# The retention branch of a hybrid decoder trunk: chunks of 64 tokens in place of 128

## The chip, the cores and the metric

The kernel runs on one core of a Trainium2 chip. The metric is device time in microseconds for one launch: the whole trunk, two layers, from the first instruction to the last. Three runs of the kernel before took 1705.79 to 1705.82 us, with a median of 1705.8 us. The engines are TensorE (PE, with PEld for its weight loads), VectorE (DVE), ScalarE (ACT), GpSimd (POOL) and SyncE (SP), which issues the DMAs.

## The reference, cut to what matters

Each layer normalizes `x`, projects it once into four causal mixers (forgetting attention, gated linear attention "GLA", retention, Mamba-2 "SSD") and a gate for each, sums the gated mixers, projects the sum out, and follows with a SwiGLU block. Sequence length is 512, the model width 1024. The change concerns retention alone: four heads of 64, float32.

```python
def retention_chunked(q, k, v, log_gamma):          # CHUNK = 64
    scores = einsum('bcthd,bcshd->bchts', qf, kf) * decay
    o_intra = einsum('bchts,bcshv->bcthv', scores, vf)
    kv = einsum('bcshd,sh,bcshv->bchdv', kf, k_w, vf)
    def step(state, kv_c):
        return state * chunk_decay[:, None, None] + kv_c, state
    _, s_in = lax.scan(step, s0, moveaxis(kv, 1, 0))
    o_inter = einsum('bcthd,th,bchdv->bcthv', qf, q_w, s_in)
    return o_intra + o_inter
```

The decay of retention is a fixed power of a constant per head, so the same output comes from chunks of any length: within a chunk by masked scores, across chunks by a state that is decayed and added to once per chunk.

## The kernel before

Everything is feature-major: 128 partitions hold features (or, in value tiles, tokens), 512 tokens lie along the free axis. Four heads of 64 are two pairs `j`, and `half` is the head within the pair, so that a head lies on 64 of the 128 partitions.

The large projections (`w_in`, the gates, the up projections, `w_out`, both halves of the SwiGLU) are split into a high and a low part in a one-pass float format, and each block of 128x128 weights takes three matmuls (`mm3`, by L200 `mm`). Their weights arrive in slabs of eight blocks by DMA, are cast by ACT (`wh`, L214) and subtracted by DVE (`wl`, L215). A slab's buffers come free when the last matmul on the slab three before has run.

The small matmuls of the mixers read float32 tiles directly. A float32 matmul takes two passes of the array, and each pass has a record of its own in the trace. Matmuls whose operands lie on 64 partitions use half of the array's rows; those that write 64 partitions of PSUM use half of its columns.

The four mixers are generators (`ssd`, `gla`, `ret`, `fox`) that `drain` runs one after the other. At each `yield` the drain emits projection work from a list (`fill`) worth some microseconds, so that projections stand between the dependent steps of a mixer. From this order of emission a scheduler with a simulated timeline sets the order of instructions on each engine when the program is built. On the chip each engine keeps that order and waits on semaphores.

Retention in the kernel before, in four chunks of 128 tokens:

- rotary: `rq` and `rk` are turned (L936 to L940).
- scores: sixteen matmuls per layer, each 64 features deep, 128 keys by 128 queries. DVE multiplies four tiles of 128x512 by a decay table out of PSUM (L957).
- keys to token-major: eight transposes (L964), times a decay (L966).
- contributions: twelve matmuls per layer, 128 tokens deep, 64x64 out, into one PSUM tile for three chunks.
- states: two copies (L980) and two steps of four scalar_tensor_tensor instructions on 64x64 (L983) write three states to `sbd`.
- output: sixteen value matmuls (128 tokens deep, 64 by 128 out) and then six matmuls of the state (128 deep, 128x128, both heads of a pair at once by a block-diagonal `sbd`) onto the same PSUM tiles. Both are called "inter" and "values" below: values are `v` times scores, inter is state times decayed query (`qd`).
- `headnorm` squares, sums, normalizes and multiplies by the gate.

GLA, which runs just before, is written in chunks of 64 already: 28 contributions of 64x64, seven states by L902 and L905, and inter matmuls on 64x64.

Of the kernel before, what the change touches and what calls it, by code (L numbers as in the profile page):

```python
# [14 lines left out]
ALU = mybir.AluOpType  # L15
# [3 lines left out]
P = 128  # L19
# [3 lines left out]
NB = S // P  # L23
# [3 lines left out]
NH = 4  # L27
# [28 lines left out]
def _const_parts():  # L56
# [4 lines left out]
    for m in range(P):  # L61
        if m % 64 < 32:
            perm[m + 32, m] = -1.0
        else:
            perm[m - 32, m] = 1.0
    dret = np.zeros((P, NH, P))
    rel = i[None, :] - i[:, None]
    for h in range(NH):
        dret[:, h, :] = np.where(rel >= 0, np.exp(np.maximum(rel, 0) * LOGG[h]), 0.0) * 0.125
    qdec = np.zeros((P, 2, P))  # L70
    for j in range(2):
        for half in range(2):
            qdec[64 * half:64 * half + 64, j, :] = np.exp((i + 1.0) * LOGG[2 * j + half])[None, :]
    kdec = np.exp((P - 1.0 - i)[:, None] * LOGG[None, :]) * 0.125
    inv = (10000.0 ** (-np.arange(32) / 32.0))[i % 32][:, None]
# [59 lines left out]
def trunk(ctx: ExitStack, tc: tile.TileContext, keys, qkeys, xin, pos, wst, wsq, par, ext, cst, out):  # L135
# [54 lines left out]
    def MX():  # L190
        return px.tile([P, S], F32, tag="mx", name=nm("mx"))
# [4 lines left out]
    def chunked(ap, n=NB):  # L196
        return ap.rearrange("p (c t) -> p c t", c=n)

    def mm(o, l, r, start, stop):
        T.matmul(o, lhsT=l, rhs=r, start=start, stop=stop, skip_group_check=True)  # L200
# [140 lines left out]
    def C(n):  # L341
        o, w = CONST_OFF[n]
        return cs[:, o:o + w]
# [10 lines left out]
    Uf = U.bitcast(F32)  # L354
    dret = C("dret").rearrange("p (h t) -> p h t", h=NH)
    qdec = C("qdec").rearrange("p (h t) -> p h t", h=2)
# [94 lines left out]
    def layer(l, n1, scope):  # L451
# [175 lines left out]

        def headnorm(pos_, gain, gates_, res):
            sq = []
# [15 lines left out]
            for j, t in enumerate(r):  # L645
                act(out=t, in_=t, func=AF.Exp, scale=-0.5)
                newton(t, pn[j], 64)
                V.scalar_tensor_tensor(out=t, in0=pos_[j], scalar=gain, in1=t, op0=ALU.mult, op1=ALU.mult)
                V.tensor_tensor(out=t, in0=t, in1=gates_[j], op=ALU.mult)
                res[j] = split_tile(t)  # L650
# [276 lines left out]
        def ret():  # L927
# [15 lines left out]
            for j in range(2):  # L943
                t = TT()
                G.tensor_tensor(out=chunked(t), in0=chunked(rq[j]), in1=qdec[:, j].unsqueeze(1).broadcast_to([P, NB, P]), op=ALU.mult)
                qd.append(t)
            ms = {}
            for j in range(2):
                pa = [MX(), MX()]
                for tb in range(NB):  # L950
                    ts = slice(tb * P, (tb + 1) * P)
                    for half in range(2):
                        hs = slice(64 * half, 64 * half + 64)
                        mm(pa[half][:, ts], rk[j][hs, ts], rq[j][hs, ts], True, True)
                for half, ps in enumerate(pa):
                    t = TT()
                    V.tensor_tensor(out=chunked(t), in0=chunked(ps), in1=dret[:, 2 * j + half].unsqueeze(1).broadcast_to([P, NB, P]), op=ALU.mult)  # L957
                    ms[j, half] = t
                yield
            kt = []  # L960
# [7 lines left out]
            yield  # L968
            ps = MX()
            pv = ps[:, :384].rearrange("p (c j n) -> p c j n", c=3, j=2)  # L970
            for c in range(3):
                for j in range(2):
                    for half in range(2):
                        hd = 2 * j + half
                        mm(pv[64 * half:64 * half + 64, c, j], kt[j][:, c * P + 64 * half:c * P + 64 * half + 64], rv[0][:, c, hd * 64:(hd + 1) * 64], True, True)
            for c in range(3):
                for half in range(2):
                    hs = slice(64 * half, 64 * half + 64)
                    if c == 0:
                        V.tensor_copy(out=sbd[hs, 0, :, hs], in_=pv[hs, 0])  # L980
                    else:
                        for j in range(2):
                            V.scalar_tensor_tensor(out=sbd[hs, c, j, hs], in0=sbd[hs, c - 1, j, hs], scalar=float(np.exp(P * LOGG[2 * j + half])), in1=pv[hs, c, j], op0=ALU.mult, op1=ALU.add)  # L983
            yield
            pos_ = [MX(), MX()]
            for j, po in enumerate(pos_):
                for c in range(NB):
                    ts = slice(c * P, (c + 1) * P)
                    for half in range(2):
                        hd = 2 * j + half  # L990
                        mm(po[64 * half:64 * half + 64, ts], rv[0][:, c, hd * 64:(hd + 1) * 64], ms[j, half][:, ts], c == 0, False)
            for j, po in enumerate(pos_):
                for c in range(1, NB):
                    ts = slice(c * P, (c + 1) * P)
                    mm(po[:, ts], sbd[:, c - 1, j], qd[j][:, ts], False, c == NB - 1)
            yield
            yield from headnorm(pos_, PR("rn"), gates["r"][2:], yc)


# [553 lines left out]
```

## Time and profile before

| | |
|---|---|
| median of 3 runs | 1705.8 us |
| the profiled execution, whole | 1704.74 us |
| span of its instructions | 1703.0 us |
| PE busy in the span | 1695.2 us |
| DVE busy | 1213.9 us |
| ACT busy | 862.3 us |
| granted TensorE clock, mean | 1.000 |

The profiled execution's own time is 1.7 us more than its span and 1.1 us less than the median of the timed runs. A row of the timeline gives the start of an instruction or of a run of like instructions, how long it lasted to the modelled end of the last, and in brackets the idle time before it on its engine. Matmuls are pipelined: the distance between two starts is what the array took, the duration beside it is longer and overlaps the next. Layer 0's retention runs at 255 to 271 us, layer 1's at 1101 to 1117 us.

### The profile page before, as it was taken

To read this page: it belongs to the slowest core of one execution; us is meant where nothing else is said; L and a number is where in the kernel's file an instruction comes from. 1 tells how busy PE (TensorE), PEld (TensorE's weight loads), DVE (VectorE), ACT (ScalarE), POOL (GpSimd) and SP (SyncE) were. 2 spreads that over 40 slices of the span, in tenths; PEclk is the share of its full clock that TensorE was granted. 3 is DMA by queue.
4 is the path that set the end of the run, shared out by engine and by line. 5 is a ranking of instruction groups with operands and counts; after the bars stand their busy time and mean duration, and the time that the engine had idled before them with its cause. 6 is when DMAs were issued, how large, how long until landed. Compare 5 with 4: busy or idle time off the path is not lost.

```text
span 1703.0 us, 25205 instructions
## 1 busy us (share of the span) xinstructions
PE 1695.2 (100%) x10174; PEld 1476.3 (87%) x10174; DVE 1213.9 (71%) x1692; ACT 862.3 (51%) x1188; POOL 218.1 (13%) x221
## 2 busy tenths in 40 slices
PE   9999999999999999999999999999999999999999
PEld 8878888888888999998988788888888889999998
DVE  6867676777677676676777766767776677767666
ACT  5425543546357555464544354435554474655543
POOL 3021220022101010101020212201221010101010
PEclk9999999999999999999999999999999999999999
DMA  6322222222235657575333222322222366665743
GB/s 208 112 72 73 80 75 87 87 87 76 86 99 159 181 135 190 130 192 117 89 108 112 64 75 76 98 76 87 79 83 87 99 176 161 152 175 138 189 105 108
DMA packets 54838, 195.02 MB, mean 115 GB/s; under 512 B 6208, under 2 KB 6848, under 8 KB 54720
## 3 DMA queue, kind: packets, MB, share of 16 engines
q1 hardware_dynamic: 45936, 161.93, 30.2%
q0 software_dynamic: 8640, 31.46, 10.3%
q8 instruction: 80, 1.31, 0.3%
q14 instruction: 38, 0.31, 0.1%
q10 hardware_dynamic: 144, 0.00, 0.0%
HBM read 191.28 MB, written 2.10 MB: 114 GB/s over the span
## 4 chain that ended last, share of the span: by engine, by line
PE 97%; DVE 2%; ACT 1%; issue 1%; POOL 0%; DVEq 0%; POOLq 0%
PE mm L200 65%; PE mx L200 31%; PE mx L1092 1%; DVE t L846 0%; DVE f L1436 0%; DVE x L1437 0%; ACT wh L214 0%; DVE wl L215 0%; PE mx L702 0%; DVE t L852 0%; ACT t L238 0%; DVE t L380 0%; ACT L233 0%; ACT g L238 0%; DVE t L1181 0%
## 5 line engine op out<-in xcount | busy, mean ns | idle before, releaser
L214 ACT CAST wh<-wr 128x1024 fp32r<-128x1024 f32 (+1 forms) x239 | 250.1, 1047 | 359.3 <-PE mm L200 200.1
L200 PE MATMUL mm<-xh,wh 128*128 128x512 f32 (+1 forms) x1184 | 428.4, 362 | 1.4 <-DVE t L1181 0.9
L200 PE MATMUL mm<-xh,wl 128*128 128x512 f32 (+1 forms) x1184 | 427.6, 361 | 0.0
L200 PE MATMUL mm<-xl,wh 128*128 128x512 f32 (+1 forms) x1184 | 427.4, 361 | 0.0
L215 DVE TENSOR_TENSOR wl<-wr,wh 128x1024 fp32r<-128x1024 f32 (+1 forms) x219 | 283.7, 1296 | 108.6 <-ACT wh L214 106.5
L200 PEld LDWEIGHTS mm<-xh,wh 128*128 128x128 f32 x1184 | 222.5, 188 | 36.1 <-DVE t L1181 1.8
L200 PEld LDWEIGHTS mm<-xl,wh 128*128 128x128 f32 x1184 | 222.4, 188 | 34.5 <-issue 1.5
L200 PEld LDWEIGHTS mm<-xh,wl 128*128 128x128 f32 x1184 | 222.5, 188 | 33.9 <-issue 0.6
L200 PE MATMUL mm<-t,wh 128*128 128x512 f32 x448 | 140.3, 392 | 0.0
L200 PE MATMUL mx<-xl,wh 128*128 128x256 f32 (+1 forms) x448 | 137.8, 309 | 0.0
L200 PE MATMUL mx<-xh,wh 128*128 128x256 f32 (+1 forms) x448 | 135.3, 310 | 0.0
L1300 POOL DMA_DIRECT2D wl<-in_wsq_dram x60 | 51.9, 864 | 517.4 <-ACT wl L1299 384.0
L200 PE MATMUL mx<-f,wh 128*128 128x512 f32 x352 | 108.2, 390 | 0.0
L200 PE MATMUL mm<-f,wh 128*128 128x512 f32 (+1 forms) x360 | 106.4, 385 | 0.0
L200 PEld LDWEIGHTS mm<-t,wh 128*128 128x128 f32 x448 | 83.2, 188 | 17.3
L215 DVE TENSOR_TENSOR l<-rq,wh 128x1024 fp32r<-128x1024 f32 x60 | 73.2, 1220 | 32.5 <-ACT wh L214 18.6
L200 PE MATMUL mx<-xh,wl 128*128 128x256 f32 (+1 forms) x288 | 91.2, 327 | 0.0
L200 PEld LDWEIGHTS mx<-xh,wh 128*128 128x128 f32 x448 | 84.2, 188 | 5.2 <-ACT wh L214 0.2
L200 PEld LDWEIGHTS mx<-xl,wh 128*128 128x128 f32 x448 | 84.1, 188 | 5.1
L200 PE MATMUL mm<-t,wl 128*128 128x512 f32 x224 | 87.4, 390 | 0.0
L214 ACT CAST wh<-rq 128x1024 fp32r<-128x1024 f32 x60 | 62.9, 1049 | 43.8 <-PE mm L200 21.5
L200 PEld LDWEIGHTS mm<-f,wh 128*128 128x128 f32 x360 | 67.1, 188 | 13.3
(277 smaller groups left out, 3431.2 us busy)
## 6 DMA issues: line engine op xcount, KB each, us to landing
wr<-in_wst_dram SPq DMA_DIRECT2D x217, 512.0 KB, 3.5
rq<-in_wsq_dram SPq DMA_DIRECT2D x60, 512.0 KB, 5.6
wl<-in_wsq_dram POOLq DMA_DIRECT2D x60, 512.0 KB, 7.2
wr<-in_wsq_dram SPq DMA_DIRECT2D x20, 512.0 KB, 6.7
out_dram<-x SPq DMA_DIRECT2D x7, 256.0 KB, 2.1
x<-in_x_dram SPq DMA_DIRECT2D x3, 512.0 KB, 7.9
x<-in_x_dram SPq DMA_DIRECT2D x2, 256.0 KB, 4.0
wr<-in_wst_dram SPq DMA_DIRECT2D x2, 256.0 KB, 4.2
```

The source lines that it names most:

```text
L200: T.matmul(o, lhsT=l, rhs=r, start=start, stop=stop, skip_group_check=True)
L214: seen["copy"] = A.copy(out=hi, in_=src)
L215: V.tensor_tensor(out=lo, in0=src, in1=hi.bitcast(F32), op=ALU.subtract)
L1092: T.transpose(ps[:, W:W + P], zs[qb][:, kb * P:(kb + 1) * P], ident)
L1300: G.dma_start(out=lo, in_=wsq[j], accum_op=ALU.add)
```

## The change

Retention is computed in eight chunks of 64 tokens. The two chunks of a block of 128 tokens lie on the two halves of the partitions ("parity"). Scores become 32 matmuls of 64 deep and 64x64 per layer, which write both chunks of a block side by side, so that DVE's decay multiplication covers two tiles in place of four. Contributions become 28 matmuls of 64 deep and 64x64; states become seven (two copies, six steps of four L998 instructions). Values become 32 matmuls of 64 deep and 64x64. Inter becomes 28 matmuls of 128 deep and 64x64, onto PSUM tiles that are ordered by parity. `headnorm` reads these, and its last multiplication writes the tokens back into their order, in two halves. The constant tables shrink. After the states the generator yields 2 in place of 1.

```diff
-    dret = np.zeros((P, NH, P))
-    rel = i[None, :] - i[:, None]
+    dret = np.zeros((P, 2, 2, 64))
+    rel = i[None, :64] - i[:, None] % 64
...
-    kdec = np.exp((P - 1.0 - i)[:, None] * LOGG[None, :]) * 0.125
+    kdec = np.exp((63.0 - i % 64)[:, None] * LOGG[None, :]) * 0.125
...
+        def cells(t):
+            return t.rearrange("p (j c t) -> p j c t", j=2, c=NB)
...
+                if parity:
+                    for i in range(2):
+                        g = gates_[i].rearrange("p (c n t) -> p c n t", c=NB, n=2)[:, :, j]
+                        V.tensor_tensor(out=g, in0=cells(t)[:, i], in1=g, op=ALU.mult)
+                        if j:
+                            res[i] = split_tile(gates_[i])
+                    continue
...
-            ms = {}
+            pa = [MX(), MX()]
             for j in range(2):
-                pa = [MX(), MX()]
                 for tb in range(NB):
-                    ts = slice(tb * P, (tb + 1) * P)
-                    for half in range(2):
-                        hs = slice(64 * half, 64 * half + 64)
-                        mm(pa[half][:, ts], rk[j][hs, ts], rq[j][hs, ts], True, True)
-                for half, ps in enumerate(pa):
-                    t = TT()
-                    V.tensor_tensor(out=chunked(t), in0=chunked(ps), in1=dret[:, 2 * j + half].unsqueeze(1).broadcast_to([P, NB, P]), op=ALU.mult)
-                    ms[j, half] = t
-                yield
+                    for par_ in range(2):
+                        rs = slice(64 * par_, 64 * par_ + 64)
+                        ts = slice(tb * P + 64 * par_, tb * P + 64 * par_ + 64)
+                        for half in range(2):
+                            hs = slice(64 * half, 64 * half + 64)
+                            mm(cells(pa[half])[rs, j, tb], rk[j][hs, ts], rq[j][hs, ts], True, True)
+            ms = []
+            for half, ps in enumerate(pa):
+                t = cells(TT())
+                V.tensor_tensor(out=t, in0=cells(ps), in1=dret[:, half].unsqueeze(2).broadcast_to([P, 2, NB, 64]), op=ALU.mult)
+                ms.append(t)
+            yield
...
-            for c in range(3):
+            pk = [MX(), MX()]
+            for tb in range(NB):
+                for j in range(2):
+                    for par_ in range(2 if tb < NB - 1 else 1):
+                        rs = slice(64 * par_, 64 * par_ + 64)
+                        pv = pk[par_].rearrange("p (c j n) -> p c j n", c=NB, j=2)
+                        for half in range(2):
+                            hd = 2 * j + half
+                            mm(pv[64 * half:64 * half + 64, tb, j], kt[j][rs, tb * P + 64 * half:tb * P + 64 * half + 64], rv[0][rs, tb, hd * 64:(hd + 1) * 64], True, True)
+            for n in range(7):
+                pv = pk[n % 2].rearrange("p (c j n) -> p c j n", c=NB, j=2)[:, n // 2]
+                for half in range(2):
+                    hs = slice(64 * half, 64 * half + 64)
+                    if n == 0:
+                        V.tensor_copy(out=sbd[hs, 0, :, hs], in_=pv[hs])
+                    else:
+                        for j in range(2):
+                            V.scalar_tensor_tensor(out=sbd[hs, n, j, hs], in0=sbd[hs, n - 1, j, hs], scalar=float(np.exp(64 * LOGG[2 * j + half])), in1=pv[hs, j], op0=ALU.mult, op1=ALU.add)
+            yield 2
+            pos_ = [MX(), MX()]
+            for j in range(2):
+                for tb in range(NB):
+                    for par_ in range(2):
+                        rs = slice(64 * par_, 64 * par_ + 64)
+                        for half in range(2):
+                            hd = 2 * j + half
+                            mm(cells(pos_[par_])[64 * half:64 * half + 64, j, tb], rv[0][rs, tb, hd * 64:(hd + 1) * 64], ms[half][rs, j, tb], j == 0 and tb == 0, False)
+            for n in range(1, 8):
+                cs_ = slice(n * 64, (n + 1) * 64)
                 for j in range(2):
                     for half in range(2):
...
-                    mm(po[:, ts], sbd[:, c - 1, j], qd[j][:, ts], False, c == NB - 1)
-            yield
-            yield from headnorm(pos_, PR("rn"), gates["r"][2:], yc)
+                        hs = slice(64 * half, 64 * half + 64)
+                        mm(cells(pos_[n % 2])[hs, j, n // 2], sbd[:, n - 1, j, hs], qd[j][:, cs_], False, j == 1 and n > 5)
+            yield
+            yield from headnorm(pos_, PR("rn"), gates["r"][2:], yc, True)
```

The scheduler sets a new order around these steps, and elsewhere next to none. On PE, layer 0, the end of the values and the inter matmuls of before (`sbd` is the states, `lf` a small sum for the attention branch, 128x256 the projection for its values):

```order
1259 L200 MATMUL mx_2438<-t_2297,v_1506 64x128
1260 L200 MATMUL mx_2438<-t_2299,v_1506 64x128
1261 L200 MATMUL mx_2461<-lf_748,cr 128x16
1262 L200 MATMUL mx_2461<-lfp_767,cr 128x16
1263 L200 MATMUL mx_2437<-t_2236,sbd_162 128x128
1264 L200 MATMUL mx_2438<-t_2238,sbd_162 128x128
1265 L200 MATMUL mm_2466<-wl_2408,xh_134 128x256
1266 L200 MATMUL mx_2437<-t_2236,sbd_162 128x128
1267 L200 MATMUL mx_2438<-t_2238,sbd_162 128x128
1268 L200 MATMUL mm_2466<-wh_2407,xl_135 128x256
```

The same place in the changed kernel, from the first contributions to the last inter matmuls (14 rows of contributions, 32 of values and 14 of inter follow each other with nothing between):

```order
1246 L200 MATMUL mm_2546<-wl_2451,xh_134 128x256
1247 L200 MATMUL mm_2546<-wh_2450,xl_135 128x256
1248 L200 MATMUL mx_2358<-v_1506,t_2316 64x64 x2
...
1261 L200 MATMUL mx_2358<-v_1506,t_2323 64x64 x2
1262 L200 MATMUL mx_2480<-t_2274,v_1506 64x64
...
1293 L200 MATMUL mx_2481<-t_2276,v_1506 64x64
1294 L200 MATMUL mx_2481<-t_2236,sbd_162 64x64 x2
1295 L200 MATMUL mx_2481<-t_2238,sbd_162 64x64 x2
...
1307 L200 MATMUL mx_2481<-t_2238,sbd_162 64x64 x2
1308 L200 MATMUL mx_2542<-lf_748,cr 128x16
1309 L200 MATMUL mx_2542<-lfp_767,cr 128x16
1310 L200 MATMUL mm_2546<-wh_2450,xh_134 128x256
```

Ten projection matmuls of 256 columns stood ahead of the contributions of before; now three do, and the other seven stand behind the inter matmuls, where the inter matmuls themselves had some among them.

On DVE, before, around the states of layer 0 (L497 takes a projection out of PSUM):

```order
284 L497 TENSOR_TENSOR t_2435<-mm_2404,n_321 128x512
285 L215 TENSOR_TENSOR wl_2536<-wr_2533,wh_2535 128x1024
286 L980 COPY sbd_162<-mx_2381 64x2x64 x2
287 L983 SCALAR_TENSOR_TENSOR sbd_162<-sbd_162,mx_2381 64x64 x8
288 L1018 COPY cq_776<-mx_2461 128x16
```

And in the changed kernel:

```order
282 L497 TENSOR_TENSOR t_2478<-mm_2447,n_321 128x512
283 L215 TENSOR_TENSOR wl_2617<-wr_2614,wh_2616 128x1024
284 L995 COPY sbd_162<-mx_2358 64x2x64 x2
285 L998 SCALAR_TENSOR_TENSOR sbd_162<-sbd_162,mx_2359 64x64 x4
286 L998 SCALAR_TENSOR_TENSOR sbd_162<-sbd_162,mx_2358 64x64 x4
287 L998 SCALAR_TENSOR_TENSOR sbd_162<-sbd_162,mx_2359 64x64 x4
288 L998 SCALAR_TENSOR_TENSOR sbd_162<-sbd_162,mx_2358 64x64 x4
289 L998 SCALAR_TENSOR_TENSOR sbd_162<-sbd_162,mx_2359 64x64 x4
290 L998 SCALAR_TENSOR_TENSOR sbd_162<-sbd_162,mx_2358 64x64 x4
291 L215 TENSOR_TENSOR t_2605<-t_2602,t_2604 128x512
```

The states stand at the same place behind the same two instructions, with 24 steps in place of 8. On PE the eight transposes of the keys, which stood in two fours among projections, now follow the scores directly.

## Rows read from the trace of the kernel before

**Rows 1.** The page: busy time of each engine with its share of the span and its instructions, and the chain that ended last by engine.

```profile
PE 1695.2 (100%) x10174; PEld 1476.3 (87%) x10174; DVE 1213.9 (71%) x1692; ACT 862.3 (51%) x1188; POOL 218.1 (13%) x221
...
PE 97%; DVE 2%; ACT 1%; issue 1%; POOL 0%; DVEq 0%; POOLq 0%
```

**Rows 2.** The timeline of PE in layer 0, around the retention scores (start us, duration us, engine, line, operation, out<-in, count).

```profile
255.40 0.39 PE L200 MATMUL mm<-xh,wl 128*128 128x512 f32 x1
255.72 2.06 PE L200 MATMUL mx<-t,t 64*128 64x128 f32 x32
257.70 0.50 PE L200 MATMUL mm<-xh,wh 128*128 128x512 f32 x1
258.04 0.39 PE L200 MATMUL mm<-xl,wh 128*128 128x512 f32 x1
258.27 0.40 PE L200 MATMUL mm<-xh,wl 128*128 128x512 f32 x1
...
260.79 0.60 PE L964 MATMUL mx<-cs,t 128*128 128x128 f32 x4
...
261.46 0.39 PE L200 MATMUL mm<-xh,wl 128*128 128x512 f32 x1
```

**Rows 3.** The same view a little later: contributions (`mx<-v,t`), values (`mx<-t,v`), the small sums and the inter matmuls (`mx<-t,sbd`).

```profile
264.21 0.28 PE L200 MATMUL mm<-wh,xh 128*128 128x256 f32 x1
...
264.44 0.28 PE L200 MATMUL mm<-wh,xl 128*128 128x256 f32 x1
...
265.48 0.34 PE L200 MATMUL mx<-v,t 128*64 128x64 f32 x4
...
266.39 0.22 PE L200 MATMUL mx<-v,t 128*64 128x64 f32 x1
266.45 1.85 PE L200 MATMUL mx<-t,v 128*64 128x128 f32 x29
268.23 0.39 PE L200 MATMUL mx<-lf,cr 128*128 128x16 f32 x2
...
268.70 0.69 PE L200 MATMUL mx<-t,sbd 128*128 128x128 f32 x4
...
270.71 0.28 PE L200 MATMUL mm<-wh,xh 128*128 128x256 f32 x1
```

**Rows 4.** The timeline of PE in GLA of layer 0, where 64x64 tiles run in the kernel before: the contributions (28 matmuls, 56 records), and the same row asked for at two instants, where the count is of the records under way then.

```profile
199.63 1.68 PE L200 MATMUL mx<-v,t 64*64 64x64 f32 x56
...
200.62 0.40 PE L200 MATMUL mx<-v,t 64*64 64x64 f32 x8
...
200.38 0.40 PE L200 MATMUL mx<-v,t 64*64 64x64 f32 x14
```

**Rows 5.** GLA's states on DVE and its inter matmuls on PE in layer 0, and what the view of the tile `sbd` says of waits (us, times).

```profile
201.47 5.57 DVE L905 SCALAR_TENSOR_TENSOR sbd<-sbd,dc,mx 64x64 f32<-64x64 f32 x22
...
207.23 1.92 PE L200 MATMUL mx<-t,sbd 64*64 64x64 f32 x56
...
  DVE sbd L905: 0.3, 2
```

**Rows 6.** The timeline of DVE over the states of layer 0, with the idle time before an instruction and what ended it.

```profile
264.48 0.69 DVE L497 TENSOR_TENSOR t<-mm,n 128x512 f32<-128x512 f32 x1 [0.86 <-PE mm L200]
265.26 1.23 DVE L215 TENSOR_TENSOR wl<-wr,wh 128x1024 fp32r<-128x1024 f32 x1
266.66 0.61 DVE L980 COPY sbd<-mx 64x128 f32<-64x128 f32 x2 [0.18 <-PE mx L200]
267.30 1.51 DVE L983 SCALAR_TENSOR_TENSOR sbd<-sbd,mx 64x64 f32<-64x64 f32 x8
```

**Rows 7.** The timeline of ACT beside it.

```profile
264.17 1.05 ACT L214 CAST wh<-wr 128x1024 fp32r<-128x1024 f32 x1 [7.53 <-PE mm L200]
270.51 0.60 ACT L238 ACTIVATE t<-mx 128x512 f32<-128x512 f32 x1 [5.28 <-PE mx L200]
```

**Rows 8.** Busy time by window: us, then busy time and count of PE, PEld, DVE, ACT, POOL, the granted TensorE clock, DMA share and GB/s.

```profile
271.00:300.00 29.00, 29.00 (x167) 25.48 (x167) 18.99 (x26) 12.58 (x19) 0.52 (x1) 1.00 0.23 73
...
1701.00:1702.00 1.00, 0.00 (x0) 0.00 (x0) 0.00 (x0) 0.00 (x0) 0.00 (x0) 1.00 0.60 197
1702.00:1703.00 1.00, 0.00 (x0) 0.00 (x0) 0.00 (x0) 0.00 (x0) 0.00 (x0) 0.67 0.00 0
```

**Rows 9.** The timeline of PE further on: the next matmuls that read what the normalization of retention's output makes.

```profile
285.85 0.64 PE L200 MATMUL mx<-t,cr 128*128 128x512 f32 x2
```

**Rows 10.** Layer 1: DVE and PE at the states and the matmuls around them.

```profile
1112.83 0.61 DVE L980 COPY sbd<-mx 64x128 f32<-64x128 f32 x2 [0.18 <-PE mx L200]
1113.47 1.51 DVE L983 SCALAR_TENSOR_TENSOR sbd<-sbd,mx 64x64 f32<-64x64 f32 x8
...
1110.37 0.28 PE L200 MATMUL mm<-wh,xh 128*128 128x256 f32 x1
...
1116.87 0.28 PE L200 MATMUL mm<-wh,xh 128*128 128x256 f32 x1
```

**Rows 11.** The timeline of PE at the run's beginning and its end.

```profile
1.39 4.63 PE L200 MATMUL mm<-t 128*128 128x128 f32 x20 [1.39 <-POOL t L336]
...
1699.19 0.28 PE L200 MATMUL mm<-f,wl 128*128 128x256 f32 x1
```

More of the change, by code (lines that the diff above doesn't have):

```diff
@@ L65, in _const_parts @@
             perm[m - 32, m] = 1.0
-    dret = np.zeros((P, NH, P))
-    rel = i[None, :] - i[:, None]
+    dret = np.zeros((P, 2, 2, 64))
+    rel = i[None, :64] - i[:, None] % 64
     for h in range(NH):
-        dret[:, h, :] = np.where(rel >= 0, np.exp(np.maximum(rel, 0) * LOGG[h]), 0.0) * 0.125
-    qdec = np.zeros((P, 2, P))
+        dret[:, h % 2, h // 2] = np.where(rel >= 0, np.exp(np.maximum(rel, 0) * LOGG[h]), 0.0) * 0.125
+    qdec = np.zeros((P, 2, 64))
     for j in range(2):
         for half in range(2):
-            qdec[64 * half:64 * half + 64, j, :] = np.exp((i + 1.0) * LOGG[2 * j + half])[None, :]
-    kdec = np.exp((P - 1.0 - i)[:, None] * LOGG[None, :]) * 0.125
+            qdec[64 * half:64 * half + 64, j, :] = np.exp((i[:64] + 1.0) * LOGG[2 * j + half])[None, :]
+    kdec = np.exp((63.0 - i % 64)[:, None] * LOGG[None, :]) * 0.125
     inv = (10000.0 ** (-np.arange(32) / 32.0))[i % 32][:, None]
@@ L354, in trunk @@
     Uf = U.bitcast(F32)
-    dret = C("dret").rearrange("p (h t) -> p h t", h=NH)
+    dret = C("dret").rearrange("p (n j t) -> p n j t", n=2, j=2)
     qdec = C("qdec").rearrange("p (h t) -> p h t", h=2)
@@ L626, in stacked_rows, with headnorm @@
             return r
-        def headnorm(pos_, gain, gates_, res):
+        def cells(t):
+            return t.rearrange("p (j c t) -> p j c t", j=2, c=NB)
+        def headnorm(pos_, gain, gates_, res, parity=False):
             sq = []
@@ L944, in ret @@
                 t = TT()
-                G.tensor_tensor(out=chunked(t), in0=chunked(rq[j]), in1=qdec[:, j].unsqueeze(1).broadcast_to([P, NB, P]), op=ALU.mult)
+                G.tensor_tensor(out=chunked(t, 8), in0=chunked(rq[j], 8), in1=qdec[:, j].unsqueeze(1).broadcast_to([P, 8, 64]), op=ALU.mult)
                 qd.append(t)
-            ms = {}
+            pa = [MX(), MX()]
             for j in range(2):
-                pa = [MX(), MX()]
                 for tb in range(NB):
-                    ts = slice(tb * P, (tb + 1) * P)
-                    for half in range(2):
-                        hs = slice(64 * half, 64 * half + 64)
-                        mm(pa[half][:, ts], rk[j][hs, ts], rq[j][hs, ts], True, True)
-                for half, ps in enumerate(pa):
-                    t = TT()
-                    V.tensor_tensor(out=chunked(t), in0=chunked(ps), in1=dret[:, 2 * j + half].unsqueeze(1).broadcast_to([P, NB, P]), op=ALU.mult)
-                    ms[j, half] = t
-                yield
+                    for par_ in range(2):
[10 more added lines that the diff above has]
+            yield
             kt = []
@@ L968, in ret @@
             yield
-            ps = MX()
-            pv = ps[:, :384].rearrange("p (c j n) -> p c j n", c=3, j=2)
-            for c in range(3):
+            pk = [MX(), MX()]
[7 more added lines that the diff above has]
+                            mm(pv[64 * half:64 * half + 64, tb, j], kt[j][rs, tb * P + 64 * half:tb * P + 64 * half + 64], rv[0][rs, tb, hd * 64:(hd + 1) * 64], True, True)
@@ L972, in ret @@
                 for j in range(2):
                     for half in range(2):
[L974 to L983, printed above, removed]
@@ L984, in ret @@
-            yield
[L985 to L994, printed above, removed]
-                    mm(po[:, ts], sbd[:, c - 1, j], qd[j][:, ts], False, c == NB - 1)
```

## The prediction

> **What bounds the kernel now.** I read the page first, then the timelines of PE, DVE and ACT around layer 0's retention, then layer 1's, then GLA, which already works in 64x64 tiles. The page shows PE busy for 1695.2 us of a span of 1703.0, and 97% of the chain that ended last on PE [rows 1]. So PE sets the time: whatever shortens its work or makes it wait is paid in full, and work on DVE (71%) or ACT (51%) counts only where PE waits for it. The reader is to see in the timeline of PE that retention's small matmuls stand among projections with no idle time before them [rows 2, 3].
>
> All times below are on layer 0's clock.
>
> **Scores.** Between the projection at 255.40 and the one at 258.04 stand the scores and one more projection. A projection's spacing is 0.23 us (258.04 to 258.27), so the scores cost 2.64 - 2 x 0.23 = 2.18 us [rows 2]. Sixteen float32 matmuls are 32 records, two at a time on the two row halves, that is 16 steps of 128 columns. A step is read from the values: 29 records in 1.85 us, the last 0.27 its own tail, 14 steps of 0.113 [rows 3]. So 16 x 0.113 = 1.81, and 0.37 is entering and leaving.
>
> The 32 new matmuls are 64 records over four quarters of the array, since `half` picks the row half and `par_` the column half. A step of 64 columns is bounded by GLA's contributions: 56 records in pairs, (1.68 - 0.22) / 27 = 0.054, a little low because two row halves ran together at their change [rows 4]; GLA's inter gives (1.92 - 0.22) / 27 = 0.063, a little high for a wait in it [rows 5]. I take 0.058. Whether four quarters run at once: in GLA 8 records are under way where one row half works, and 14 at the instant where the row half changes [rows 4]. That speaks for four, so 16 steps x 0.058 + 0.37 = 1.30, a gain of 0.88 us per layer. If only two ran at once, 32 x 0.058 + 0.37 = 2.23, a loss of 0.05.
>
> The Trainium skill ("TensorE: Matmul & The Clock Gate", section "Wait — 56ns, not 53.3ns?") says that the distance between two matmul starts never falls below about 25 ns. By it the 64 records take at least 1.6 us and the gain would be 0.2 instead of 0.88. The trace does not bear it out for tiles side by side: 14 records under way, each about 0.22 long, are one in 16 ns.
>
> **Transposes.** Each four cost 261.46 - 260.79 - 0.23 = 0.44, together 0.88 [rows 2]; eight in a row at the 0.113 of a step are 0.90. No change.
>
> **Contributions, states, values, inter.** I measure from E = 264.21, where the 512-column projections end and the 256-column ones begin [rows 3]; both orders have that point, with the same DVE work hanging on it.
>
> Before, E to the regular stretch at 270.71 takes 6.50 us, which includes 15 matmuls of 256 columns at 0.117 (264.21 to 264.44 is two).
>
> In the changed order DVE comes to the states by the same two instructions: the projection that ended at E is taken out (264.48), then the slab split of L215 (265.26 + 1.23 = 266.49) [rows 6], whose cast on ACT began at 264.17 when PE released the slab [rows 7]. PE has by then run three 256-column matmuls and the 56 records of contributions (16 steps of 0.058 in the fuller row half): 264.56 + 0.30 + 0.93 = 265.8. So DVE, not PE, starts the states, at 266.5. The two copies take 0.64 to the first step (266.66 to 267.30), and 8 steps take 1.51 [rows 6], 0.189 each. The 24 take 4.53 and end at 266.5 + 0.64 + 4.53 = 271.67. GLA's steps, with a scalar read from memory, need 5.57 / 22 = 0.253 [rows 5]; that is the upper bound and would add 1.5 us. Nothing in the trace runs a dependent step faster than 0.189; for a lower bound I allow a tenth, 0.45 us less. I take 0.189, since constant and shape are those of L998.
>
> PE meanwhile has the values alone: 16 steps of 0.058, done by about 266.8. Then it meets the inter matmuls, and as PE runs in order nothing behind them, the `lf` sums and all projections, can pass. Inter step n needs state n, which comes every 4 x 0.189 = 0.76 us, and works 0.23 for it. This is the new wait: a first piece of 0.3 and six of about half a microsecond, some 3.5 us per layer, for PEld on `sbd`, from DVE. The row of the 0.3 us in GLA, twice, is the same wait in small: there seventeen projections stood between contributions and values [rows 5].
>
> After the last step at 271.67: 0.05 for the signal (the last contribution ends at 266.39 + 0.22, the copy starts at 266.66 [rows 3, 6]), 0.23 for the last four inter matmuls, 0.14 until the next form starts (the values' last record starts at 268.03 by its 0.27, `lf` at 268.23: 0.20, of which 0.11 is that record's own step, and 0.05 that I add for the first pass after a wait), so `lf` at 272.1. Then `lf` and its fellow, 0.47 (268.23 to 268.70), and the other 12 matmuls of 256 columns, 1.40, with 0.1 on return: 274.1 where before it was 270.71 [rows 3]. A loss of 3.4 us per layer. Contributions, values and the longer inter (28 matmuls are 28 steps of 0.058, 1.6 us) all lie inside the wait, so that their own gain or loss doesn't show.
>
> **What is hidden.** DVE saves two multiplications of 128x512 and gains 16 state steps (16 x 0.189 = 3.0 us) and two more, half as wide, in `headnorm`. Beyond the states themselves it has 10 us idle in the 29 us behind [rows 8]. ACT's squares started at 270.51 and start later now [rows 7]; the next matmul on them is at 285.85 [rows 9], so some 12 us cover it, and if that cover were gone the cost would be at most the 3.4 again. The smaller tables and the decayed queries on POOL change no wait that PE has.
>
> **Sum.** Per layer -0.88 + 0 + 3.4 = +2.5 us. Layer 1's rows repeat layer 0's, with 6.50 us from 1110.37 to 1116.87 and the same two durations on DVE [rows 6, 10], so for two layers +5.0. The profiled execution took 1704.74, so 1709.7 for it; it ran 1.1 under the median of 1705.8, so for the median 1710.8 us, or +0.29%. What a measurement of this kernel can tell from no change is about 0.2%, that is 3.4 us.
>
> **Rivals.**
>
> *The states are covered.* If PE found the states ready (by an earlier start of DVE, or if PE were slower on the 64x64 tiles than I reckon), only PE's own work counts. Contributions and values took 268.23 - 265.48 = 2.75 [rows 3] and would take 2 x 0.93 + 0.3 = 2.16; inter, six matmuls of two passes at 0.113, 1.36, becomes 1.62 + 0.2 for a change of form. With the scores that is -0.88 - 0.59 + 0.46 = -1.0 per layer: 1703.8 us, not slower. For it: DVE is 29% idle over the span. Against it: the order of DVE puts the steps behind a split of 1.23 us that waits for the same E, and 24 dependent steps are 4.5 us against 0.9 us of values. It decides from the point where some 4 us of other matmuls stood between. Chance 0.12.
>
> *Quarters don't run together.* Then scores gain nothing (+0.05) while the wait stays: 2 x 3.45 = 6.9, or 1712.7 us. For it: whole stretches on four quarters do not exist in the trace. Against it: the 14 records under way [rows 4]. Chance 0.14, the skill's 25 ns included, which by 64 x 0.025 + 0.37 = 1.97 would give 2 x (3.4 - 0.2) = 6.4 and 1712.2.
>
> *The clock falls.* PE would work some 0.23 of every 0.76 us for 4.5 us. The granted clock was 1.00 throughout, which is 2.4 GHz, and at the end of the run still 1.00 from 1701 to 1702 and 0.67 from 1702 to 1703, when the last matmul had started at 1699.19 [rows 8, 11]; so it stood through 2.5 us without any matmul, and the wait has none longer than about 0.6. At the beginning 20 passes of 128 columns took 4.63 us, 0.21 each after the first, twice the later 0.113 [rows 11]: the level of 1.2 GHz. If the clock fell near the end of the wait and needed as long to return, half of 4.6 us would be lost, twice: +4.6, or 1715.4 us. The Trainium skill (same page, section "What's actually happening") says that the throttled clock is the default and that activity releases it; how much counts as activity no row here shows. Chance 0.08.
>
> *My forecast*, PE waits for the states and the quarters run together: 0.66, with 1709 to 1713 as its own range.
>
> **Chances and range.** Slower by over 0.2% (above 1709.2) follows from nearly all of the forecast (0.58 of its 0.66; its lower end reaches 1709 and a tenth off the steps costs 0.9) and from two rivals, together 0.80. Within 0.2%: the rest of the forecast and most of the covered states, 0.16. Faster by over 0.2% needs more than -3.4 us, which no case gives; 0.04 for what I don't see. The range reaches down past the lower bound of the steps and part of the way to the covered states, 1707, and up to GLA's slower steps (1713.9) with a part of the clock's case, 1714.5.
>
> **What would show it.** In the profile after: idle time of PE or PEld for DVE `sbd` L998, some 3.5 us per layer, near 0 before; L998 with 48 instructions at about 217 ns, in 4.5 us per layer; the scores as 64 records in about 1.3 us between projections; the projections at the same spacing of 0.23, the clock at 1.00. The wait is wrong if PE's idle for `sbd` stays under 1 us; the quarters if the scores still take 2 us; the sum if another wait appears behind the states, at the next matmuls of 285.85 or in the attention branch.

## The result and the profile after

The changed kernel takes 1708.79 us (median of 21 runs, 1708.26 to 1710.29). The kernel before took 1705.29 us beside it (21 runs, 1704.68 to 1707.22). The ratio is 1.0021 with a 95% interval of 1.0015 to 1.0027, so it is slower by 2.6 to 4.6 us. The profiled execution took 1709.5 us with a span of 1707.8, against 1704.74 and 1703.0.

The page of the changed kernel, first the busy times and then the chain by engine; it answers to [rows 1]:

```profile
PE 1699.4 (100%) x10454; PEld 1477.9 (87%) x10454; DVE 1216.0 (71%) x1724; ACT 862.8 (51%) x1188; POOL 218.4 (13%) x221
...
PE 95%; DVE 2%; issue 1%; ACT 1%; DMA 1%; SPq 0%; DVEq 0%; POOLq 0%
```

PE still counts as busy all the time, with 280 more records, and 95% of the chain is still its own. By these lines alone one would say that it has more work. The timeline of PE in layer 0 (start, duration, engine, line, operation, shapes, count; two passes are two records) says otherwise:

```profile
255.69 0.39 PE L200 MATMUL mm<-xh,wl 128*128 128x512 f32 x1
256.01 1.16 PE L200 MATMUL mx<-t,t 64*64 64x64 f32 x64
257.10 1.09 PE L976 MATMUL mx<-cs,t 128*128 128x128 f32 x8
...
263.52 0.28 PE L200 MATMUL mm<-wh,xh 128*128 128x256 f32 x1
...
264.94 1.10 PE L200 MATMUL mx<-t,v 64*64 64x64 f32 x62
266.13 5.19 PE L200 MATMUL mx<-t,sbd 128*64 128x64 f32 x56
271.25 0.40 PE L200 MATMUL mx<-lf,cr 128*128 128x16 f32 x2
...
273.22 0.28 PE L200 MATMUL mm<-wh,xh 128*128 128x256 f32 x1
...
277.23 0.28 PE L200 MATMUL mm<-wl,xh 128*128 128x256 f32 x1
```

Two things stand out. The 64 score records take 1.16 us where 32 records of 128 columns took 2.06 [rows 2]. And inter takes 5.19 us, while the 62 records of the values above it, of the same number of columns, take 1.10. The stretches, with E the first projection of 256 columns and the 16th of them as its end, as in the prediction:

| layer 0 | before [rows 2, 3] | after | difference |
|---|---|---|---|
| last projection ahead of the scores to E | 264.21 - 255.40 = 8.81 | 263.52 - 255.69 = 7.83 | -0.98 |
| E to the 16th projection of 256 columns | 270.71 - 264.21 = 6.50 | 273.22 - 263.52 = 9.70 | +3.20 |

Layer 1 repeats it: from 1112.34 to 1122.03 are 9.69, where before had 6.50 [rows 10]. Its rows in the changed kernel, by the same view:

```profile
1112.34 0.28 PE L200 MATMUL mm<-wh,xh 128*128 128x256 f32 x1
...
1122.03 0.28 PE L200 MATMUL mm<-wh,xh 128*128 128x256 f32 x1
```

The difference of the scores is the same there, 1112.34 - 1104.51 = 7.83 where before had 1110.37 - 1101.56 = 8.81.

Two layers at +2.22 are 4.44, more than the 3.5 by which the medians differ. Some 50 us behind retention the changed kernel gains a little: PE of the kernel before stands idle there, once per layer, for a multiplication on DVE (L1181, the gate), and PE of the changed kernel doesn't. The same matmul before and after:

```profile
323.73 0.50 PE L200 MATMUL mm<-xh,wh 128*128 128x512 f32 x1 [0.45 <-DVE t L1181]
```

```profile
325.74 0.50 PE L200 MATMUL mm<-xh,wh 128*128 128x512 f32 x1
```

Layer 1 has it again (1169.90, with 0.45 of idle time before it, against 1174.55 with none). So a layer costs 2.22 - 0.45 = 1.77 more, and two layers the 3.5 of the medians. Why this idle time went no run settles; the control of run 8, in chunks of 128, still has it, and runs 2, 3, 5, 6, 7 and 9 don't. The two profiled executions differ by 4.8 us, because two things come to the 3.5 in them: 0.29 had arisen before the scores of layer 0 (255.69 against 255.40), and about 1.0 arises near 800 us, between the two retentions, where projections stand 0.12 us apart in this execution and 0.113 in that of the kernel before. The profiled executions of runs 3 and 6 do not have the second.

DVE beside it, the answer to [rows 6]:

```profile
263.72 0.69 DVE L497 TENSOR_TENSOR t<-mm,n 128x512 f32<-128x512 f32 x1 [1.33 <-PE mm L200]
264.57 1.23 DVE L215 TENSOR_TENSOR wl<-wr,wh 128x1024 fp32r<-128x1024 f32 x1 [0.16 <-ACT wh L214]
265.71 0.60 DVE L995 COPY sbd<-mx 64x128 f32<-64x128 f32 x2
266.34 4.60 DVE L998 SCALAR_TENSOR_TENSOR sbd<-sbd,mx 64x64 f32<-64x64 f32 x24
```

The steps run from 266.34 to 270.94, and inter from 266.13 to 271.32: the two rows cover the same time. The view of the waits (us in total, times, longest) and the granted clock by window (the column behind POOL's):

```profile
PEld mx L200 <- DVE sbd L998: 2.3, 12, 0.2
```

```profile
264.00:268.00 4.00, 3.79 (x144) 3.29 (x144) 3.66 (x13) 0.54 (x1) 0.00 (x0) 1.00 0.23 61
268.00:272.00 4.00, 3.77 (x44) 2.94 (x41) 2.73 (x17) 1.32 (x3) 0.00 (x0) 1.00 0.20 78
```

The wait has the name that was foretold, but the view shows only 2.3 us for both layers. It counts the weight loads' idle time alone. Between two state steps the modelled ends of the matmuls reach over part of the gap, so that PE counts as busy in it; PE's own idle time has no entry for `sbd` at all. The length of the row, 5.19 us, is the better reading, once a run shows how long the same row is without the wait.

### The profile page after: what moved, and what is told of

Same layout as the page of the kernel before. It is cut to its first block, busy times and chain, and to the rows that moved or that the text cites. A ratio compares the mean times of both kernels' runs of the same rounds, so it can differ in the third digit from the quotient of the medians.

```text
span 1707.8 us, 25799 instructions
## 1 busy us (share of the span) xinstructions
PE 1699.4 (100%) x10454; PEld 1477.9 (87%) x10454; DVE 1216.0 (71%) x1724; ACT 862.8 (51%) x1188; POOL 218.4 (13%) x221
## 4 chain that ended last, share of the span: by engine, by line
PE 95%; DVE 2%; issue 1%; ACT 1%; DMA 1%; SPq 0%; DVEq 0%; POOLq 0%
PE mm L200 64%; PE mx L200 30%; PE mx L1110 1%; DVE sbd L998 0%; ACT wh L214 0%; DMA wl<-in_wsq_dram 0%; DMA x<-in_x_dram 0%; DVE wl L215 0%; DVE f L1454 0%; DVE x L1455 0%; PE mx L712 0%; ACT L233 0%; DVE t L856 0%; PE mx L976 0%; ACT g L238 0%
```

## The experiments

The theory: PE stands in inter behind the chain of 24 state steps on DVE, which costs 3.2 us per layer, and the scores give 0.98 back because four quarters of the array run at once.

**1. Later values and inter.** More of the other work is emitted between the states and the values.

```diff
-            yield 2
+            yield 3
             pos_ = [MX(), MX()]
```

> The values and inter come 45 projections of 256 columns later (the yield after the states gives way to more of the other work); contributions and the DVE states stay where they were. Theory A (PE waits in inter for the chain of 24 dependent DVE steps): the 45 projections are 5.3 us of work that runs while the 4.6 us chain does, so inter finds its states ready, its row shrinks from 5.2 us to about 1.8, and the time falls to 2 x 1.0 under the kernel before (scores and contributions keep their gain): 1703.3 us, 1702.5 to 1704.3, where after is 1708.8 and before 1705.3. Rival B (the 56 records of inter and the other small tiles take that time by themselves, wherever they stand): inter keeps some 5 us and the time stays within 0.7 of 1708.8.

Measured: 1723.64 us (4 runs), ratio 1.0109 (1.0095 to 1.0122) to the kernel before: far slower, as neither theory had it. Yet at the place itself theory A holds. The timeline of PE:

```profile
270.97 1.16 PE L200 MATMUL mx<-t,v 64*64 64x64 f32 x64
272.06 1.85 PE L200 MATMUL mx<-t,sbd 128*64 128x64 f32 x56
```

Inter's own work is 1.85 us, so 5.19 - 1.85 = 3.34 us of the row were wait. The loss stands over 100 us later, in the attention branch. The waits of this run, and its windows there:

```profile
PEld mx L200 <- ACT t L214: 11.3, 2, 5.7
```

```profile
385.00:390.00 5.00, 0.26 (x1) 0.26 (x2) 3.49 (x5) 4.61 (x8) 0.00 (x0) 0.75 0.22 64
390.00:395.00 5.00, 5.00 (x14) 3.96 (x15) 4.94 (x9) 0.13 (x1) 3.50 (x5) 0.57 0.10 41
```

A `yield` draws its projections from one list that retention and the attention branch share. What retention used more of was missing later, in the attention branch: PE stood for 5.7 us in each layer, and in the 5 us after it the granted clock was 0.57. The run moved the wait and didn't remove it; it says nothing of what the cover is worth.

**2. The chain doubled.** The result is the same, with two dependent instructions where there was one.

```diff
-V.scalar_tensor_tensor(out=sbd[hs, n, j, hs], in0=sbd[hs, n - 1, j, hs], scalar=float(...), in1=pv[hs, j], op0=ALU.mult, op1=ALU.add)
+V.tensor_scalar(out=sbd[hs, n, j, hs], in0=sbd[hs, n - 1, j, hs], scalar1=float(...), scalar2=None, op0=ALU.mult)
+V.tensor_tensor(out=sbd[hs, n, j, hs], in0=sbd[hs, n, j, hs], in1=pv[hs, j], op=ALU.add)
```

> Each state step is written as two DVE instructions, a multiplication and an addition in place of one that does both, so that the chain has 48 dependent steps for the same result. Theory A: 24 more steps at about 0.19 us lie in the wait in full, +4.5 us per layer, 1717.8 us (1716 to 1719.5), and the inter row grows from 5.2 to some 9.7 us. Rival B (inter is bound by its own work on PE): DVE has idle time for 9 us more over the run, so within 0.7 us of 1708.8.

Measured: 1720.21 us (4 runs), ratio 1.0086 (1.0071 to 1.0102). The direction is theory A's; the size is above its range. The timeline of PE now shows the states as pieces of inter, and behind them projections of 256 columns at a wider spacing:

```profile
267.62 0.86 PE L200 MATMUL mx<-t,sbd 128*64 128x64 f32 x8 [0.44 <-DVE sbd L999]
269.04 0.86 PE L200 MATMUL mx<-t,sbd 128*64 128x64 f32 x8 [0.56 <-DVE sbd L999]
...
276.74 0.41 PE L200 MATMUL mm<-wh,xl 128*128 128x256 f32 x1
...
280.37 0.38 PE L200 MATMUL mm<-wl,xh 128*128 128x256 f32 x1
```

```profile
268.00:272.00 4.00, 2.47 (x23) 1.77 (x24) 3.62 (x24) 0.00 (x0) 0.00 (x0) 0.79 0.27 112
272.00:276.00 4.00, 3.66 (x28) 3.00 (x28) 3.12 (x19) 1.39 (x3) 0.00 (x0) 0.50 0.00 0
276.00:280.00 4.00, 4.00 (x20) 4.00 (x21) 1.38 (x4) 1.04 (x2) 0.52 (x1) 0.50 0.02 4
280.00:284.00 4.00, 4.00 (x33) 4.00 (x33) 0.00 (x0) 0.27 (x1) 0.00 (x0) 0.93 0.00 0
```

A state comes every 1.42 us (267.62, 269.04) instead of 4 x (4.60 - 0.22) / 23 = 0.76, and six states are 6 x 0.66 = 4.0 us more. The rest is the clock: it fell to 0.50, the level of 1.2 GHz, during the wait and came back at 280.6. Until then the projections ran at (280.37 - 276.74) / 17 = 0.214 instead of 0.118, 20 of them, 1.9 us. Together that is 5.9 per layer. From E to the 50th projection of 256 columns this run takes 283.65 - 263.89 = 19.76 and the changed kernel 277.23 - 263.52 = 13.71, which is 6.05. Two layers are 12.1; the profiled executions differ by 12.7 (this one is the slowest of its four), the medians by 1720.21 - 1708.79 = 11.4. In the changed kernel itself the same windows have 1.00 (above). The scheduler also put one of the `lf` sums in front of the last state's matmuls here, so that PE's order is not quite that of the changed kernel.

**3. Scores with two quarters at a time.** The 32 matmuls are the same, in another order.

```diff
-            for j in range(2):
-                for tb in range(NB):
-                    for par_ in range(2):
+            for par_ in range(2):
+                for j in range(2):
+                    for tb in range(NB):
```

> The 32 score matmuls alone are put in another order: all 16 of the even chunks first (two quarters of the array in use), then the 16 of the odd chunks. Theory A (the scores gained 0.98 us per layer because four quarters run at once): with two at a time the 64 records need 32 steps of 0.058 and what entering costs, so the scores take about 2.1 us where the changed kernel has 1.16, +0.95 per layer, +1.9 in all: 1710.7 us. Rival B (the gain is that of fewer columns, each record being as fast on its own in any order): 1.2 us for the scores again and 1708.8.

Measured: 1709.53 us (7 runs), ratio 1.0028 (1.0017 to 1.0039): by the time alone not to be told from the changed kernel's 1.0021. The timeline of PE decides it:

```profile
255.24 0.39 PE L200 MATMUL mm<-xh,wl 128*128 128x512 f32 x1
255.56 1.91 PE L200 MATMUL mx<-t,t 64*64 64x64 f32 x64
257.40 1.10 PE L976 MATMUL mx<-cs,t 128*128 128x128 f32 x8
```

The same 64 records take 1.91 us in place of 1.16, and the transposes start 2.16 after the last projection instead of 1.41. Four quarters at once are worth 0.75 us per layer, less than the 0.95 expected. The averages, (1.91 - 0.22) / 31 = 0.055 for a step of two records and (1.16 - 0.22) / 15 = 0.063 for one of four, mislead. Record by record, the first step lasts 0.107 us in both runs and every other one 0.058, whether it holds two records or four; the records of one step start within 0.02 us. Run 3 needs less than 32 steps because at the change from even to odd chunks three of its pairs ran beside another pair.

**4. The kernel before with later values.** Meant as a control for the first run, with `yield 3` for its `yield` at the same place.

> The control for the first run: the same change of the yield after the states in the kernel before, where there are 8 steps of states and PE stands nowhere for them. Theory A: no wait to cover, within 0.7 us of the kernel before, 1705.3. Rival B (this place of the values is better for any version, whatever the states do, by less contention or by what follows): some 2 to 5 us under the kernel before.

Measured: 1716.06 us (5 runs), ratio 1.0066 (1.0054 to 1.0079). Neither theory had it, and the waits show the first run's trouble again (in the kernel before, the first of the two is 1.8 us and the second isn't listed):

```profile
PEld mm L200 <- DVE t L1181: 4.5, 6, 1.5
PEld mm L200 <- ACT t L214: 4.5, 2, 2.2
```

So a kernel without any wait for states loses too when retention draws more of the common work. Both runs need a version that draws no more.

**5. Later values, same budget.** As the first run, but the `yield` behind inter goes.

```diff
-            yield 2
+            yield 3
             pos_ = [MX(), MX()]
...
                         mm(cells(pos_[n % 2])[hs, j, n // 2], sbd[:, n - 1, j, hs], qd[j][:, cs_], False, j == 1 and n > 5)
-            yield
             yield from headnorm(pos_, PR("rn"), gates["r"][2:], yc, True)
```

> As in the first run the values and inter come 45 projections of 256 columns later, but the yield behind inter is taken out for it, so that retention uses up no more of the other work than the changed kernel does; behind these 45 projections PE's order is that of the changed kernel, word for word. Theory A (the changed kernel loses 3.2 us per layer by the wait for the states and gains 0.98 by the scores; the first run lost elsewhere, because the attention branch ran out of other work): inter's row is 1.85 us as in the first run, no wait of some microseconds for ACT appears later, and the time is 2 x 0.98 under the kernel before: 1703.2 us (1702.2 to 1704.2). Rival B (whatever comes after values that stand later is late too, as in the first run): no gain over the changed kernel, 1708 or more.

Measured: 1702.26 us (11 runs) against 1705.03 before, ratio 0.9984 (0.9975 to 0.9993). It is faster than both kernels, than the one before by 0.16%. The timeline of PE:

```profile
255.28 0.39 PE L200 MATMUL mm<-xh,wl 128*128 128x512 f32 x1
...
263.11 0.28 PE L200 MATMUL mm<-wh,xh 128*128 128x256 f32 x1
...
270.58 1.16 PE L200 MATMUL mx<-t,v 64*64 64x64 f32 x64
271.67 1.85 PE L200 MATMUL mx<-t,sbd 128*64 128x64 f32 x56
...
273.68 0.28 PE L200 MATMUL mm<-wl,xh 128*128 128x256 f32 x1
```

273.68 is the 50th projection of 256 columns, 10.57 behind E. In the changed kernel the 50th starts at 277.23, 13.71 behind E; the cover is worth 3.14 per layer, 6.3 in all, and the medians differ by 6.5.

**6. The chain halved.** Nothing is moved on PE; DVE does both halves in one step.

```diff
-for half in range(2):
-    ...
-    V.scalar_tensor_tensor(out=sbd[hs, n, j, hs], in0=sbd[hs, n - 1, j, hs], scalar=float(...), in1=pv[hs, j], ...)
+V.scalar_tensor_tensor(out=sbd[:, n, j, :64], in0=sbd[:, n - 1, j, :64], scalar=qdec[:, j, 63:64], in1=pv[:, j], ...)
...
-mm(cells(pos_[n % 2])[hs, j, n // 2], sbd[:, n - 1, j, hs], qd[j][:, cs_], ...)
+mm(cells(pos_[n % 2])[hs, j, n // 2], sbd[:, n - 1, j, :64], qd[j][half][:, cs_], ...)
```

> The chain with 12 steps in place of 24: a step does both halves at once, 128x64, with its decay read per partition; the two copies become one. So that inter can use states without the zero blocks, the decayed queries are made as four tiles, each with the other half zero, by POOL. PE's order stays that of the changed kernel. Theory A: 12 steps at about 0.25 (GLA's, with a scalar from memory) and one copy of 0.3 take 3.4 us where the chain took 5.2, so the wait falls by some 1.8 us per layer, inter's row from 5.2 to some 3.4, and the time to 1705.2 (1704 to 1706.8). Rival B (inter is late for another reason, such as the queries of POOL or its own records): 1708.8 or, if POOL's longer work is waited for, more.

Measured: 1703.52 us (11 runs), ratio 0.9991 (0.9982 to 1.0000), faster than expected. DVE, and then PE:

```profile
265.43 0.28 DVE L997 COPY sbd<-mx 128x128 f32<-128x128 f32 x1
265.75 2.39 DVE L1000 SCALAR_TENSOR_TENSOR sbd<-sbd,cs,mx 128x64 f32<-128x64 f32 x12
```

```profile
265.86 2.67 PE L200 MATMUL mx<-t,sbd 128*64 128x64 f32 x56
```

Chain and inter shrink together, the chain by 0.30 + 2.21 and inter by 2.52. Two layers are 5.0; the medians differ by 5.3.

A step of 128x64 with its scalar read from memory comes every (2.39 - 0.28) / 11 = 0.192 us, as often as one of 64x64 with a constant does on average. But that average has two lengths in it. The first four L998 of the changed kernel, each asked for at its own instant; the code does two steps on one half of the partitions and then two on the other:

```profile
266.34 0.21 DVE L998 SCALAR_TENSOR_TENSOR sbd<-sbd,mx 64x64 f32<-64x64 f32 x1
266.48 0.20 DVE L998 SCALAR_TENSOR_TENSOR sbd<-sbd,mx 64x64 f32<-64x64 f32 x1
266.71 0.23 DVE L998 SCALAR_TENSOR_TENSOR sbd<-sbd,mx 64x64 f32<-64x64 f32 x1
266.86 0.22 DVE L998 SCALAR_TENSOR_TENSOR sbd<-sbd,mx 64x64 f32<-64x64 f32 x1
```

The same for GLA's steps in the kernel before, which alternate in the same way and read their scalar from memory:

```profile
201.47 0.27 DVE L905 SCALAR_TENSOR_TENSOR sbd<-sbd,dc,mx 64x64 f32<-64x64 f32 x1
201.66 0.27 DVE L905 SCALAR_TENSOR_TENSOR sbd<-sbd,dc,mx 64x64 f32<-64x64 f32 x1
201.97 0.29 DVE L905 SCALAR_TENSOR_TENSOR sbd<-sbd,dc,mx 64x64 f32<-64x64 f32 x1
202.17 0.29 DVE L905 SCALAR_TENSOR_TENSOR sbd<-sbd,dc,mx 64x64 f32<-64x64 f32 x1
```

A step on the half of the one before it starts 0.14 us later, one on the other half 0.23; all 24 steps of layer 0 do so, by 0.14 to 0.15 and by 0.24 to 0.25. With the scalar from memory both are about 0.06 longer, 0.20 and 0.31. The 12 steps of run 6 pay for the scalar and never change the half. So the chain became shorter by fewer steps and by the changes of half that are gone; no run takes the two apart.

**7. The states unchained.** Every step reads state 0, so that no step hangs on another; the later states leave out the chunks between.

```diff
-in0=sbd[hs, n - 1, j, hs]
+in0=sbd[hs, 0, j, hs]
```

> Each state step reads the first state in place of the one before it, so that the 24 instructions no longer depend on each other; the output differs, since the states are no longer sums over all chunks before. Theory A1 (DVE's instructions cost 0.19 us each, one behind the other, whether or not they hang on each other): nothing changes, 1708.8 within 0.7. Theory A2 (the 0.19 us is mostly the wait of a step for the result before it): the spacing falls well under 0.19, the wait with it, and the time towards 1706.

Measured: 1708.32 us (10 runs), ratio 1.0021 (1.0012 to 1.0030), the same as the changed kernel. The row of DVE:

```profile
266.50 4.50 DVE L998 SCALAR_TENSOR_TENSOR sbd<-sbd,mx 64x64 f32<-64x64 f32 x24
```

4.50 us for 24 steps where the chained ones took 4.60. So it isn't the recurrence that makes the steps slow; what counts is how many there are, and how often the half changes (run 6). The chain is four chains of six side by side: in the changed kernel a step hangs on the one four places ahead of it, in run 6 on the one two places ahead. What a step would take that hangs on the one directly ahead no run shows.

**8. The control with the same budget.** In the kernel before, `yield` becomes `yield 2` and the one behind inter goes.

> The control for the fifth run, and a cleaner one than the fourth: in the kernel before, values and inter are put 38 projections of 256 columns later, and the yield behind inter is taken out, so that the attention branch keeps all of its other work. Theory A (the fifth run is faster than the kernel before by its scores, and the place of the values matters only where there is a wait for states): within 0.8 us of the kernel before, 1705.0. Rival B (this order by itself is worth the 2.8 us that the fifth run gained): some 1702.3.

Measured: 1705.94 us (11 runs) against 1705.02, ratio 1.0006 (0.9997 to 1.0015), 0.9 above where 0.8 was the bound. The timeline of PE, from E to the 50th projection of 256 columns:

```profile
264.28 0.28 PE L200 MATMUL mm<-wh,xh 128*128 128x256 f32 x1
...
265.82 0.40 PE L200 MATMUL mx<-lf,cr 128*128 128x16 f32 x2
...
275.21 0.28 PE L200 MATMUL mm<-wl,xh 128*128 128x256 f32 x1
```

That is 10.93 us. In the kernel before it is 6.50 to the 16th and 34 more at 0.118, 10.5: 0.4 more per layer, which is the 0.9. The `lf` sums have come to stand among the contributions, which may be the reason; no run tests it. The order is worth nothing by itself. The gain of run 5 is that of the changed kernel: its smaller tiles, and the 0.45 per layer of the wait for L1181, which this run still has and run 5 hasn't.

**9. Cover and short chain together.**

> The fifth run's order together with the sixth run's 12 steps of 128x64 and masked queries. Theory A (in the fifth run nothing is left of the wait): the same time as the fifth, 1702.3 within 0.5. Rival B (there is still a piece of the wait, or the shorter work of DVE helps what comes behind): 1701.5 or less.

Measured: 1702.15 us (11 runs), ratio 0.9983 (0.9974 to 0.9992), the same as run 5. Nothing of the wait was left there.

## Why the prediction was right

The direction and the mechanism were right, and 1708.79 lies within the range of 1707.0 to 1714.5; the 1710.8 was 2.0 too high. It lies just under the 1709 to 1713 that the prediction gave its own case, and under the 1709.2 where it began to count as slower by over 0.2% (the measured ratio is 1.0021, since the kernel before came out lower too). The room below 1709 was left for shorter steps and for covered states, and neither occurred; that the number is there has other reasons, under "The sum". Step by step:

- **Scores.** Forecast -0.88 per layer, measured -0.98. The step of four was forecast at 0.058 and is 0.058. Mis-sized was the entering and leaving, taken over unchanged (0.37): in the changed order scores and transposes stand in one piece, where before the array changed its form for three pieces [rows 2]. Run 3 gives 0.75 of the 0.98 to the four quarters at once. The rest is there without them as well (263.81 - 255.24 = 8.57 for 8.81 before); how much of it is the fewer pieces no run settles.
- **The floor between starts.** The 64 records stand in 1.16 us, (1.16 - 0.22) / 63 = 0.015 each. The Trainium skill ("TensorE: Matmul & The Clock Gate", section "Wait — 56ns, not 53.3ns?") states that matmul starts are never less than some 25 ns apart; an estimate from that is 1.6 us for 64 records. For tiles side by side the measurement speaks against this floor.
- **The wait.** Forecast +3.4 between E and the 16th projection, measured +3.20. The mechanism stands on runs 2, 5 and 6: a chain of twice the steps, a chain that other work covers and a chain of half the steps give +11.4 (with a part from the clock), -6.5 and -5.3 us against the changed kernel. The copies start at 265.71, 2.19 after E for a forecast of 2.3. Last step's end: 270.94, 7.42 after E for 7.46. `lf` starts 7.73 after E for 7.9: what was mis-sized is the handing over behind the last step, 0.42 forecast and 271.25 - 270.94 = 0.31 measured.
- **The view that was to show it.** The 3.5 us per layer of PEld idle for L998 were not there: 2.3 for both layers. By the prediction's own words ("The wait is wrong if PE's idle for `sbd` stays under 1 us") 1.15 per layer was nearly enough to call the wait wrong, and PE itself shows none. The size was right and the view the wrong one: inter's row, 5.19 against 1.85 without the wait, gives 3.34 per layer.
- **GLA's slower steps as the upper bound.** The reason given, a scalar read from memory, holds: at equal halves GLA's steps stand some 0.06 us further apart than L998 (run 6), and 24 x 0.06 is the 1.5 of the prediction. That nothing runs a dependent step faster than 0.189 doesn't hold. That figure is an average over steps that start 0.14 and 0.24 apart; the average was right here because the 24 steps change the half as often as the 8 did.
- **What is hidden.** The squares' results are read at 288.36 where it was 285.85 [rows 9], 2.51 later, which is the 2.22 and the 0.29. No new wait stands behind the states. An old one went (L1181), and the prediction had no term for it.
- **The sum.** +5.0 forecast, 3.5 by the medians. Of the 1.5 between them 0.6 are the 0.2 of the wait and the 0.1 of the scores, twice, and 0.9 are the 0.45 per layer of the wait that went. The other 0.5 of the 2.0 is the kernel before, which was taken at 1705.8 from three runs and is 1705.29 over 21.

The rivals. *Covered states* did not happen, but run 5 made them happen. Its stretch from the last projection ahead of the scores to the 50th of 256 columns is 273.68 - 255.28 = 18.40. Before, the 16th and 34 more at 0.118 make 270.71 + 4.0 - 255.40 = 19.3. That is -0.9 per layer where the rival had -1.0. With the 0.45 of the wait for L1181 it is 2 x 1.35 = 2.7, and the medians give -2.8, with an interval from -4.3 to -1.2. *Quarters that don't run together* fell by run 3. *The clock* held at 1.00 in the changed kernel, and run 2 shows that it is near: with twice the steps it fell within the wait. The price put on it, 2.3 per layer, was close to the 1.9 measured in run 2.

## What to carry to other kernels

Cutting chunks in half makes the matmuls cheaper where they fill four quarters of the array, but it multiplies the small state steps on another engine (here from 8 to 24 per layer); count these instructions and look for what PE can do meanwhile, because an engine that works in order stands in the middle of the branch. Here the finer chunks paid (1702.3 instead of 1705.0 us) only once 45 projections stood between contributions and values. With steps that did two heads at once the gain, 1703.5 instead of 1705.0, lies at the edge of the interval. Where small steps go to the two halves of the partitions in turn, the starts of run 6 suggest an order with fewer changes of half; no run tries it. Work moved in front of a wait is taken from somewhere: in run 1 it was missing 100 us later, and the wait there cost more than the one removed.

## What the runs showed of the hardware

- Small DVE steps (scalar_tensor_tensor, 64x64, out of PSUM) start 0.14 us apart on the same half of the partitions and 0.24 where the half changes (L998, changed kernel); with the scalar from memory 0.20 and 0.31 (GLA's L905); at 128x64 with the scalar from memory 0.19 throughout (run 6).
- Taking away the dependence on the step four places ahead left 24 of them at 4.50 us in place of 4.60 (run 7).
- Float32 records of 64 columns come in steps of 0.058 us, with two or with four of them side by side in a step (run 3 and the changed kernel).
- The granted clock fell to 0.50 within a wait in which PE still worked on eight records every 1.42 us, and stayed there for 4.4 us of dense projections after it, to 280.6 (run 2). With eight records every 0.76 us for 5.2 us it stayed at 1.00.
- PE may count as busy for most of a wait: 5.19 us of a row with 1.85 us of work.
